# Differential attention: score matmuls over 128 rows, the next heads' projections asked for two token tiles earlier, and the products beside the attention paced evenly

## The chip, the cores and the metric

One core of a Trainium2 chip runs the whole program. The metric is the device time of one execution in microseconds (us), the median of several runs. The engines are TensorE (PE; its weight loads are listed apart as PEld), VectorE (DVE), ScalarE (ACT), GpSimd (POOL) and SyncE (SP). Each has a queue of its own that it works through in order; semaphores join them.

## The reference

The program is two transformer blocks on 512 tokens of width 1024, all in float32. The change lies in the first block's differential attention. Of the reference, what matters here (8 heads, `hd` = 64, so each head has two query and two key vectors of 64 per token and a value of 128):

```python
q = rmsnorm(q.reshape(bsz, s, B_HEADS, 2, B_HEAD_DIM), q_norm_g[l])
k = rmsnorm(k.reshape(bsz, s, B_HEADS, 2, B_HEAD_DIM), k_norm_g[l])
...
sc = jnp.einsum('bhcqd,bhckd->bhcqk', qb, k) * scale
alibi = -slopes[:, None, None] * jnp.abs(dist)[None]
sc = jnp.where((dist >= 0)[None, None, None], sc + alibi[None, :, None], -jnp.inf)
p = jax.nn.softmax(sc, axis=-1)
a = p[:, :, 0] - lam * p[:, :, 1]
return jnp.einsum('bhqk,bhkd->bhqd', a.astype(v.dtype), v)
```

q, k and v are columns of one projection `h @ w_in`. The output gate `sigmoid(h @ w_gate + b_gate)` is needed after the attention and needs nothing of it.

## The kernel before, in words

**Precise products.** Matrix operands are split into a rounded high part and a low remainder (`split_to`, lines 232 to 239: ACT writes the high part, DVE subtracts for the low one), and a product is three matmuls (`mm3`, lines 299 to 302: high times high, high times low, low times high).

**The list of dense products.** Products with weights are put on a list, an object of class `Dense` called `dn`. An item is one weight tile of 1 MB; it is loaded by SP, split by ACT and DVE (lines 290 and 291) and used in two "groups". A group of `dense_N` is 48 matmuls of 256 columns and counts as 48 x 109 = 5232 ns, one of `dense_T` is 24 matmuls of 512 columns and counts as 24 x 216 = 5184 ns. These counts are a budget and not measured times. `dn.run(ns)` adds to a debt and emits groups until the debt is paid; `dn.until(name)` emits groups until a named item is done, whatever the debt; `dn.drain()` emits the rest. The emitted program is then put in order for each engine by a scheduler, so matmuls of a group can stand between other work.

**The projections of two heads.** `push_qkv(hp)` (line 601) lists three products of 256 columns for heads 2hp and 2hp+1: q, k and v, two groups each. `evq` normalises q or k on DVE (`group_norm`, line 366: a square on ACT, then a sum, ten small operations of `rsqrt` and a multiplication on DVE). `lay(which)` (line 617) transposes the result on PE and splits it into the tile `qk`. For one head `qk` had five slots of 512 columns on 128 partitions. Slots 0 and 1 are q of the two components c: its high part in its own 64 partitions, its low part in the other 64. Slots 2 and 3 are k of the two components: the high part in its own 64 partitions, and a copy of it in the other 64, which POOL makes with a DMA (line 631). Slot 4 holds the low parts of k, component 0 in partitions 0 to 63, component 1 in 64 to 127.

**One step of the attention.** There are 32 steps, i = 0 to 31: head h = i // 4, token tile qt = i % 4 with n = 128 (qt + 1) keys. `scores(i)` issues two matmuls for each component: line 669 over all 128 rows (q high and q low, each times k high) and line 670 over the component's own 64 rows (q high times k low). `soft` adds the position term, finds the row minimum (line 680, DVE), takes the exponential (line 682, ACT) and combines the two components (lines 685 to 688, DVE). `turn` transposes (line 381) and copies (line 695), `values` multiplies with v (line 705). On PE the step i issues scores(i), turn(i-1) and values(i-2), with a `yield` after the first two; at each yield the caller runs `dn.run`.

**What sets the order beside it.** Before the attention the projections of the first two heads are done (`until("qkv0")`). The list then holds, in this order, qkv1, gate 0, qkv2, gate 1, qkv3, gate 2, gate 3 (a gate item, `push_gate_b`, is one `dense_T` tile of two groups). Each of the yields pays 1150 ns. `scores` calls `dn.until` for the projections of a pair of heads at that pair's first step. POOL's queue also holds `bn` (line 659), the position term of one head, in two buffers: a new one waits until DVE has read the head before last.

**After it** come `up_b` (the product with w_up_b, which needs all heads), the output product, the mixture of experts, whose weight buffers are granted as the output product proceeds, and the second block.

Of the kernel before, what the change touches and what calls it, by code (L numbers as in the profile page):

```python
# [6 lines left out]
F32 = mybir.dt.float32  # L7
F32R = mybir.dt.float32r
# [8 lines left out]
S = 512  # L17
# [142 lines left out]
def _body(ctx, tc, I, out):  # L160
# [270 lines left out]
                       channel_multiplier=1)  # L431
    cols = cp.tile([128, 128], F32, name="cols")
    C = {}
    b_bc = c1.tile([128, 8, 128], F32, name="b_bc")
    wsT = c1.tile([128, 8, 128], F32, name="wsT")
    nlam = cp.tile([128, 1], F32, name="nlam")
    hb_gate = cp.tile([128, 16], F32, name="hb_gate")
    g_sub = cp.tile([128, 1], F32, name="g_sub")
# [81 lines left out]
    T2["p"] = sub(gs, "t2", 7)  # L520
    v_n = gp.tile([128, 4, 1024], F32, name="v_n")
    yaT = [gp.tile([128, 8, S], F32R, name=f"yaT{i}") for i in range(2)]
    cg = constants(gp)

    def gn2(c, q, ps):
# [75 lines left out]
    def push_qkv(hp):  # L601
        qkn = {}
        h = HQ[hp] = {}

        def evq(which):
            def ev(c, q, ps):
                x = t2("qkn", (128, 2, 4, 64))
                group_norm(ps.rearrange("p (g w) -> p g w", w=64), x.rearrange("p t g w -> p (t g) w"), 8, 64)
                qkn[which, q] = x
            return ev  # L610

        def evv(c, q, ps):
            if q == 0:
                h["vb"] = ap_.tile([128, 4, 256], F32, name="vb", tag="vb")
            act.activation(h["vb"][:, 2 * q:2 * q + 2], ps.rearrange("p (t w) -> p t w", t=2), AF.Copy)

        def lay(which):
            def f():
                dn.flush()
                if which == 0:  # L620
                    h["qk"] = ap_.tile([128, 10, S], F32R, name="qk", tag="qk")
                g = col("k_norm_g") if which else g_q
                for j in range(2):
                    ps = transpose4(lambda t: qkn[which, t // 2][:, t % 2, 2 * j:2 * j + 2].rearrange("p a b -> p (a b)"))
                    for c in range(2):
                        own, other = halves(c)
                        hi = h["qk"][:, 5 * j + 2 * which + c]
                        lo = h["qk"][own, 5 * j + 4] if which else hi[other]
                        split_to(hi[own], lo, ps[own], g[own])
                        if which:  # L630
                            pool.dma_start(hi[other], hi[own])
            return f
        dense_N(w_in, 2048 + hp * 256, 256, lambda: hT, evq(0))
        dense_N(w_in, 3072 + hp * 256, 256, lambda: hT, evq(1))
        dn.call(lay(0))
        dense_N(w_in, 4096 + hp * 256, 256, lambda: hT, evv)
        dn.call(lay(1))
        dn.call(lambda: None, f"qkv{hp}")
# [10 lines left out]
    def attention():  # L649
        st = {}  # L650
        n_steps = 32

        def scores(i):
            h, qt = divmod(i, 4)
            if qt == 0 and h % 2 == 0:
                dn.until(f"qkv{h // 2}")
            if qt == 0:
                bn = c1.tile([128, 512], F32, name="bn", tag="bn", bufs=2)
                pool.tensor_scalar(bn, dpos, slopes[h], None, op0=OP.mult)
                st["bn"] = bn  # L660
            qk = HQ[h // 2]["qk"][:, 5 * (h % 2):5 * (h % 2) + 5]
            n = 128 * (qt + 1)
            nm = max(n, 256)
            qs = slice(qt * 128, qt * 128 + 128)
            pss = []
            for c in range(2):
                own = halves(c)[0]
                ps = psa()
                pe.matmul(ps[:, :nm], qk[:, c, qs], qk[:, 2 + c, :nm], start=True, stop=False)
                pe.matmul(ps[:, :nm], qk[own, c, qs], qk[own, 4, :nm], start=False, stop=True)  # L670
                pss.append(ps)
            return pss, n, qt, st["bn"]

        def soft(a):
            pss, n, qt, bn = a
            mn, den, rd = small("mn", [128, 2], 6), small("den", [128, 2], 6), small("rd", [128, 2], 6)
            sc = []
            for c in range(2):
                s = t2("sc")
                dve.tensor_tensor_reduce(s[:, :n], pss[c][:, :n], bn[:, 384 - 128 * qt:512], 1.0, 3.0e38,  # L680
                                         op0=OP.add, op1=OP.min, accum_out=mn[:, c:c + 1])
                act.activation(s[:, :n], s[:, :n], AF.Exp, bias=mn[:, c:c + 1], scale=-1.0,
                               accum_out=den[:, c:c + 1])
                sc.append(s)
            dve.reciprocal(rd, den)
            dve.tensor_mul(rd[:, 1:2], rd[:, 1:2], nlam)
            dve.tensor_scalar(sc[0][:, :n], sc[0][:, :n], rd[:, 0:1], None, op0=OP.mult)
            dve.scalar_tensor_tensor(sc[0][:, :n], sc[1][:, :n], rd[:, 1:2], sc[0][:, :n], op0=OP.mult, op1=OP.add)
            return sc[0], n, qt

        def turn(a):
            s, n, qt = a
            pt = transpose4(lambda k: s[:, k * 128:k * 128 + 128], qt + 1)
            aT = t2("aT")
            act.activation(aT[:, :n], pt[:, :n], AF.Copy)
            return aT

        def values(i, aT):
            h, qt = divmod(i, 4)
            vb = HQ[h // 2]["vb"]  # L700
            if qt == 0:
                st["po"] = psa()
            po = st["po"]
            for kt in range(qt + 1):
                pe.matmul(po[:, qt * 128:qt * 128 + 128], aT[:, kt * 128:kt * 128 + 128],
                          vb[:, kt, (h % 2) * 128:(h % 2) * 128 + 128], start=kt == 0, stop=kt == qt)
            if qt == 3:
                on = t2("on", (128, 4, 128))
                group_norm(po.rearrange("p (g w) -> p g w", g=4), on, 4, 128)
                st["on"] = (h, on)  # L710

        def finish():
            h, on = st.pop("on")
            ps = transpose4(lambda t: on[:, t])
            act.activation(ybT[:, h], ps, AF.Copy, scale=g_sub)

        sc, aT = {}, {}
        for i in range(n_steps + 3):
            fin = "on" in st
            if i < n_steps:  # L720
                sc[i] = soft(scores(i))
            yield
            if 1 <= i <= n_steps:
                aT[i - 1] = turn(sc.pop(i - 1))
            yield
            if fin:
                finish()
            if 2 <= i <= n_steps + 1:
                values(i - 2, aT.pop(i - 2))

    push_qkv(0)
    dn.until("qkv0")
    push_qkv(1)
    push_gate_b(0)
    push_qkv(2)
    push_gate_b(1)
    push_qkv(3)
    push_gate_b(2)
    push_gate_b(3)
    for _ in attention():  # L740
        dn.run(1150.0)
    dn.drain()
    at_.close()
    hs_.close()
# [1298 lines left out]
```

## Time and profile before

| | |
|---|---|
| median of 3 runs | 1792.62 us (1791.51 to 1793.68) |
| the profiled execution, its own time | 1795.56 us |
| its span, first to last instruction | 1793.5 us |
| mean granted TensorE clock | 0.972 of full speed |
| PE busy | 1692.7 us (94% of the span) |
| PEld busy | 1373.6 us (77%) |
| DVE busy | 947.6 us (53%) |
| ACT busy | 662.1 us (37%) |
| POOL busy | 285.7 us (16%) |

Busy PE is not PE at its peak, because matmuls are pipelined: a matmul's duration in the trace is longer than its distance to the next one. What a matmul costs is read from start to start. Durations on DVE overlap a little as well. "Granted clock" is the share of the full TensorE clock of 2.4 GHz in a stretch, so 0.5 is the lower level, 1.2 GHz. The attention lies between about 248 and 482 us of the span.

### The profile page before, as it was taken

The page shows a single profiled execution, that of the slowest core. Times are in us where ns is not written, and L with a number is a line of the kernel's source. Part 1 is how long each engine was busy: PE and PEld are TensorE (multiplying, and loading weights), DVE is VectorE, ACT ScalarE, POOL GpSimd, SP SyncE. Part 2 cuts the span into 40 slices and gives each one's busy share as a digit, 9 for nine tenths or more (in the row PEclk, how much of TensorE's full clock was granted, in tenths as well). Part 3 has the DMA queues.
Part 4 walks back from the last instruction along what each step waited for, and adds up shares of the span by engine and source line. Part 5 has one row for each costly group of instructions (what it writes and reads, how often), then busy time and mean ns, then how long its engine had stood idle before and what let it go on. Part 6 is the DMA issues. An engine that isn't in the chain of part 4 may idle for free.

```text
span 1793.5 us, 24558 instructions
## 1 busy us (share of the span) xinstructions
PE 1692.7 (94%) x9766; PEld 1373.6 (77%) x9766; DVE 947.6 (53%) x2001; ACT 662.1 (37%) x1128; POOL 285.7 (16%) x276
## 2 busy tenths in 40 slices
PE   7999999999999699887799988799999999999999
PEld 7888888889789455444789876588788988888887
DVE  7642367777753411111578789964467444444221
ACT  4222244454523122122435577566523322222111
POOL 1000000000012222112200178611001111111000
PEclk9999999999999799899899999899999999999999
DMA  6223322122348899998724311121243222222240
GB/s 205 94 71 117 118 84 82 48 83 83 141 141 314 324 411 415 418 416 298 218 94 118 118 48 47 71 94 48 88 142 122 83 94 94 94 94 94 83 141 35
DMA packets 151018, 263.87 MB, mean 147 GB/s; under 512 B 11771, under 2 KB 109766, under 8 KB 146550
## 3 DMA queue, kind: packets, MB, share of 16 engines
q1 hardware_dynamic: 131542, 220.03, 34.2%
q0 software_dynamic: 12400, 33.71, 6.1%
q10 hardware_dynamic: 6960, 8.56, 1.3%
q8 instruction: 77, 1.26, 0.3%
q14 instruction: 39, 0.32, 0.1%
HBM read 248.62 MB, written 18.87 MB: 149 GB/s over the span
## 4 chain that ended last, share of the span: by engine, by line
PE 41%; DVE 7%; ACT 2%; DMA 2%; issue 1%; POOL 0%; ACTq 0%; DVEq 0%; POOLq 0%
PE pd L300 11%; PE pd L301 11%; PE pd L302 11%; DVE oa L1756 3%; PE pa L301 2%; PE pa L300 2%; PE pa L302 2%; DMA x<-y_d 2%; DVE wlo L291 1%; PE pa L381 1%; PE pa L1646 1%; ACT whi L290 1%; DVE sn L1661 0%; DVE sden L1668 0%; DVE pt L236 0%
## 5 line engine op out<-in xcount | busy, mean ns | idle before, releaser
L291 DVE TENSOR_TENSOR wlo<-wraw,whi 128x2048 fp32r<-128x2048 f32 (+1 forms) x112 | 248.8, 2221 | 192.8 <-ACT whi L290 192.1
L290 ACT ACTIVATE whi<-wraw 128x2048 fp32r<-128x2048 f32 (+1 forms) x123 | 213.1, 1735 | 345.8 <-PE pd L301 198.8
L301 PE MATMUL pd<-wlo,hT 128*128 128x256 f32 x512 | 145.5, 284 | 1.5 <-DVE wlo L291 1.5
L300 PE MATMUL pd<-whi,hT 128*128 128x256 f32 x512 | 146.0, 285 | 0.0
L302 PE MATMUL pd<-whi,hT 128*128 128x256 f32 x512 | 145.2, 284 | 0.0
L302 PE MATMUL pd<-hnT,wlo 128*128 128x512 f32 x352 | 139.4, 396 | 0.0
L300 PE MATMUL pd<-hnT,whi 128*128 128x512 f32 x352 | 139.3, 396 | 0.0
L301 PE MATMUL pd<-hnT,whi 128*128 128x512 f32 x352 | 139.2, 395 | 0.0
L300 PE MATMUL pd<-xnT,whi 128*128 128x512 f32 (+1 forms) x280 | 114.3, 408 | 0.0
L301 PE MATMUL pd<-xnT,whi 128*128 128x512 f32 (+1 forms) x280 | 113.0, 404 | 0.0
L302 PE MATMUL pd<-xnT,wlo 128*128 128x512 f32 (+1 forms) x280 | 112.9, 403 | 0.0
L1750 POOL TENSOR_TENSOR oa<-oa,ctm 128x512 f32<-128x512 f32 x60 | 91.3, 1522 | 60.5 <-ACT ctm L1749 57.0
L301 PEld LDWEIGHTS pd<-wlo,hT 128*128 128x128 f32 x512 | 97.2, 190 | 2.6 <-DVE wlo L291 1.8
L300 PEld LDWEIGHTS pd<-whi,hT 128*128 128x128 f32 x512 | 97.4, 190 | 1.2 <-issue 0.9
L302 PEld LDWEIGHTS pd<-whi,hT 128*128 128x128 f32 x512 | 97.1, 190 | 0.9 <-issue 0.4
L870 DVE SCALAR_TENSOR_TENSOR sg<-sg,pd 128x256 f32<-128x256 f32 x16 | 6.7, 421 | 165.6 <-ACT sg L869 165.6
L891 PE MATMUL pd<-mraw,xs 128*64 128x256 f32 x624 | 77.6, 401 | 11.8 <-DMA mraw<-in_w 11.6
L300 PEld LDWEIGHTS pd<-hnT,whi 128*128 128x128 f32 x352 | 66.1, 188 | 16.0
L301 PEld LDWEIGHTS pd<-hnT,whi 128*128 128x128 f32 x352 | 66.1, 188 | 15.9
L302 PEld LDWEIGHTS pd<-hnT,wlo 128*128 128x128 f32 x352 | 66.1, 188 | 15.8
L300 PE MATMUL pd<-hT,whi 128*128 128x512 f32 x192 | 77.8, 405 | 0.0
L302 PE MATMUL pd<-hT,wlo 128*128 128x512 f32 x192 | 77.7, 405 | 0.0
(546 smaller groups left out, 4059.1 us busy)
## 6 DMA issues: line engine op xcount, KB each, us to landing
mraw<-in_w SPq DMA_DIRECT2D x59, 1024.0 KB
wraw<-in_w_in SPq DMA_DIRECT2D x41, 1024.0 KB
wraw<-in_w_gate SPq DMA_DIRECT2D x19, 1024.0 KB
wraw<-in_w SPq DMA_DIRECT2D x11, 1024.0 KB
wraw<-in_w_up SPq DMA_DIRECT2D x11, 1024.0 KB
wlo<-in_w SPq DMA_DIRECT2D x10, 1024.0 KB
whi<-in_w SPq DMA_DIRECT2D x10, 1024.0 KB
wraw<-in_w_down SPq DMA_DIRECT2D x10, 1024.0 KB
```

The source lines that it names most:

```text
L290: act.activation(h[:, sl], r[:, sl], AF.Copy)
L291: (pool if i in by_pool else dve).tensor_tensor(l[:, sl], r[:, sl], raw(h[:, sl]), op=OP.subtract)
L300: pe.matmul(ps, ah, bh, start=start, stop=False)
L301: pe.matmul(ps, ah, bl, start=False, stop=False)
L302: pe.matmul(ps, al, bh, start=False, stop=stop)
L381: pe.transpose(ps[:, t * 128:t * 128 + 128], src_of(t), ident)
L870: dve.scalar_tensor_tensor(sg, sg, 1.0, hid[:, 0:256], op0=OP.add, op1=OP.mult)
L891: pe.matmul(ph[64 * m:64 * m + 64, 256 * j:256 * j + 256], XS[p][:, kt, 64 * m:64 * m + 64], wt[:, m, k], start=kt == 0, stop=kt == 7)
L1646: pe.matmul(ps[:, :nm], Q[:, 4 * g + i, qs], KS[:, br, g, x, :nm], start=x == 0, stop=x == 1)
L1750: pool.tensor_add(acc, acc, tm)
L1756: taps.append(lambda i=i: dve.scalar_tensor_tensor(acc, up[:, j, i:i + S], convw[:, i, j:j + 1], acc, op0=OP.mult, op1=OP.add))
```

## The change

The score matmul of line 670 becomes one over all 128 rows. `qk` gets six slots for each head: the low part of k has a slot for each component, in the component's own 64 partitions, and POOL's DMA copies high and low part together to the other 64. The second matmul then also adds q low times k low. The room comes from two tiles (`b_bc`, `wsT`) that now live only as long as the gating stage that reads them. The list is put as qkv1, qkv2, qkv3 and then the four gate items; a yield pays 2250 ns for the first 44 of 70 yields and 1550 ns after them. `dn.until` for the next pair is called at token tile 2 of a pair's second head, two steps before the pair begins.

```diff
-    b_bc = c1.tile([128, 8, 128], F32, name="b_bc")
-    wsT = c1.tile([128, 8, 128], F32, name="wsT")
...
+    b_bc = gp.tile([128, 8, 128], F32, name="b_bc")
+    wsT = gp.tile([128, 8, 128], F32, name="wsT")
...
-                    h["qk"] = ap_.tile([128, 10, S], F32R, name="qk", tag="qk")
+                    h["qk"] = ap_.tile([128, 12, S], F32R, name="qk", tag="qk")
...
-                        hi = h["qk"][:, 5 * j + 2 * which + c]
-                        lo = h["qk"][own, 5 * j + 4] if which else hi[other]
+                        hi = h["qk"][:, 6 * j + 2 * which + c]
+                        lo = h["qk"][own, 6 * j + 4 + c] if which else hi[other]
                         split_to(hi[own], lo, ps[own], g[own])
                         if which:
-                            pool.dma_start(hi[other], hi[own])
+                            both = h["qk"][:, 6 * j + 2 + c:6 * j + 5 + c:2]
+                            pool.dma_start(both[other], both[own])
...
-            if qt == 0 and h % 2 == 0:
-                dn.until(f"qkv{h // 2}")
+            if qt == 2 and h % 2 == 1 and h < 7:
+                dn.until(f"qkv{h // 2 + 1}")
...
-            qk = HQ[h // 2]["qk"][:, 5 * (h % 2):5 * (h % 2) + 5]
+            qk = HQ[h // 2]["qk"][:, 6 * (h % 2):6 * (h % 2) + 6]
...
             for c in range(2):
-                own = halves(c)[0]
                 ps = psa()
                 pe.matmul(ps[:, :nm], qk[:, c, qs], qk[:, 2 + c, :nm], start=True, stop=False)
-                pe.matmul(ps[:, :nm], qk[own, c, qs], qk[own, 4, :nm], start=False, stop=True)
+                pe.matmul(ps[:, :nm], qk[:, c, qs], qk[:, 4 + c, :nm], start=False, stop=True)
...
     push_qkv(0)
     dn.until("qkv0")
-    push_qkv(1)
-    push_gate_b(0)
-    push_qkv(2)
-    push_gate_b(1)
-    push_qkv(3)
-    push_gate_b(2)
-    push_gate_b(3)
-    for _ in attention():
-        dn.run(1150.0)
+    for hp in range(1, 4):
+        push_qkv(hp)
+    for c in range(4):
+        push_gate_b(c)
+    for i, _ in enumerate(attention()):
+        dn.run(2250.0 if i < 44 else 1550.0)
```

How this moves instructions, at two places. The first is PE at the beginning of the third pair of heads (head 4). Before, in PE's order, with `qkn` the normalised q or k, `hT` the block's input, `vb` the values and `sc` a softmax result:

```order
L302 MATMUL pd<-whi,hT_74 128x256
L381 MATMUL pa<-ident,qkn 128x128 x8
L705 MATMUL pa<-vb,aT 128x128 x3
L300 MATMUL pd<-hT_73,whi 128x512
...
L669 MATMUL pa<-qk 128x256
L670 MATMUL pa<-qk 128x256
L302 MATMUL pd<-hT_73,wlo 128x512
```

and in the changed kernel the same eight transposes of k for that pair, which now stand at token tile 1 of head 3 (the L669 and L670 rows here are that tile's scores):

```order
L302 MATMUL pd<-whi,hT_74 128x256
L705 MATMUL pa<-vb,aT 128x128 x3
L669 MATMUL pa<-qk 128x256
L670 MATMUL pa<-qk 128x256
L669 MATMUL pa<-qk 128x256
L670 MATMUL pa<-qk 128x256
L381 MATMUL pa<-ident,sc 128x128
L381 MATMUL pa<-ident,qkn 128x128 x8
L300 MATMUL pd<-whi,hT_73 128x256
```

Before, eleven matmuls of a gate product lay between the transposes of k and the first scores that need them; now three steps of the attention with their dense products lie between (L669 of head 4 follows 125 rows later).

The second place is POOL's queue over the whole attention (`bn` is the position term of a head, `qk` the copies of k). Before:

```order
L659 TENSOR_SCALAR bn<-dpos 128x512 x2
L631 DMA qk<-qk 64x512 x4
L659 TENSOR_SCALAR bn<-dpos 128x512 x2
L631 DMA qk<-qk 64x512 x4
L659 TENSOR_SCALAR bn<-dpos 128x512 x2
L631 DMA qk<-qk 64x512 x4
```

(from the terms of heads 2 and 3 on, to the copies of the last pair), and now, from the copies of the first pair on:

```order
L632 DMA qk<-qk 64x2x512 x4
L660 TENSOR_SCALAR bn<-dpos 128x512
L632 DMA qk<-qk 64x2x512 x4
L660 TENSOR_SCALAR bn<-dpos 128x512 x2
L632 DMA qk<-qk 64x2x512 x4
L660 TENSOR_SCALAR bn<-dpos 128x512 x2
L632 DMA qk<-qk 64x2x512 x4
L660 TENSOR_SCALAR bn<-dpos 128x512
```

The copies of a pair now stand ahead of the position term of the running pair's second head; before, they stood behind it. Each copy moves twice the bytes.

## Rows read from the trace of the kernel before

**Rows 1.** Windows: from:to us, length, busy PE, PEld, DVE, ACT, POOL, then PEclk, DMA share, GB/s.
```profile
247.80:482.40 234.60, 230.43 (x1475) 195.79 (x1475) 170.22 (x525) 115.18 (x240) 19.65 (x26) 0.98 0.24 72
```

**Rows 2.** Timeline of PE, token tile 3 of head 2: start, us, engine, line, what.
```profile
322.17 0.47 PE L669 MATMUL pa<-qk 128*128 128x512 f32 x1
322.57 0.50 PE L670 MATMUL pa<-qk 64*128 64x512 f32 x1
323.00 0.50 PE L669 MATMUL pa<-qk 128*128 128x512 f32 x1
323.44 0.49 PE L670 MATMUL pa<-qk 64*128 64x512 f32 x1
323.86 0.39 PE L300 MATMUL pd<-whi,hT 128*128 128x256 f32 x1
```

**Rows 3.** Timeline of the weight loads at the same place; in brackets the idle time before.
```profile
322.57 0.18 PEld L670 LDWEIGHTS pa<-qk 64*128 64x128 f32 x1 [0.24 <-issue]
323.00 0.19 PEld L669 LDWEIGHTS pa<-qk 128*128 128x128 f32 x1 [0.25 <-issue]
323.97 0.19 PEld L301 LDWEIGHTS pd<-wlo,hT 128*128 128x128 f32 x1
```

**Rows 4.** Timeline of PE, scores of 256 columns and what follows.
```profile
271.18 0.36 PE L669 MATMUL pa<-qk 128*128 128x256 f32 x1
...
272.41 0.33 PE L381 MATMUL pa<-ident,sc 128*128 128x128 f32 x1
```

**Rows 5.** Timeline of PE, second block: four score matmuls over 128 rows.
```profile
1186.51 1.09 PE L1646 MATMUL pa<-KS,Q 128*128 128x512 f32 x4
1187.44 0.39 PE L300 MATMUL pd<-omT,whi 128*128 128x512 f32 x1
```

**Rows 6.** Timeline of PE, a dense product resumed after value matmuls.
```profile
285.48 0.37 PE L301 MATMUL pd<-wlo,hT 128*128 128x256 f32 x1
285.69 0.28 PE L302 MATMUL pd<-whi,hT 128*128 128x256 f32 x1
285.81 0.28 PE L300 MATMUL pd<-whi,hT 128*128 128x256 f32 x1
```

**Rows 7.** Line 670 over the run: min/median/max ns, first and last start, forms.
```profile
L670 PE MATMUL pa<-qk x64: 377/439/686, 248.1 to 473.9; 64*128 64x256 f32 x32, 64*128 64x384 f32 x16, 64*128 64x512 f32 x16
```

**Rows 8.** Timeline of PE: where it waited; in brackets the wait and its releaser.
```profile
247.81 0.35 PE L669 MATMUL pa<-qk 128*128 128x256 f32 x1 [1.20 <-ACT qk L238]
298.75 0.66 PE L381 MATMUL pa<-ident,qkn 128*128 128x128 f32 x4 [0.39 <-DVE qkn L374]
308.11 0.36 PE L669 MATMUL pa<-qk 128*128 128x256 f32 x1 [1.78 <-DMA qk<-qk]
```

**Rows 9.** Windows of 10 us, same columns as rows 1.
```profile
280.00:290.00 10.00, 10.00 (x78) 9.03 (x77) 8.13 (x25) 5.49 (x10) 0.00 (x0) 1.00 0.32 106
290.00:300.00 10.00, 9.61 (x77) 8.96 (x76) 9.07 (x25) 7.82 (x13) 1.49 (x1) 1.00 0.01 2
300.00:310.00 10.00, 8.22 (x36) 5.87 (x34) 4.65 (x9) 3.86 (x9) 2.12 (x4) 0.97 0.59 157
310.00:320.00 10.00, 10.00 (x28) 7.25 (x29) 6.61 (x28) 2.09 (x7) 0.00 (x0) 0.52 0.00 0
```

**Rows 10.** Timeline of DVE while k of the first pair is laid out.
```profile
244.14 1.40 DVE L239 SCALAR_TENSOR_TENSOR qk<-pa,cols,qk 64x512 fp32r<-64x512 f32 x2 [4.33 <-ACT qk L238]
246.51 2.29 DVE L291 TENSOR_TENSOR wlo<-wraw,whi 128x2048 fp32r<-128x2048 f32 x1 [0.98 <-ACT whi L290]
248.84 1.43 DVE L239 SCALAR_TENSOR_TENSOR qk<-pa,cols,qk 64x512 fp32r<-64x512 f32 x2
```

**Rows 11.** Timeline of POOL at the same place.
```profile
244.65 1.07 POOL L631 DMA_DIRECT2D qk<-qk  x2 [35.07 <-ACT qk L238]
```

**Rows 12.** DMA issues: what, queue, count, KB each, median us to landing.
```profile
qk<-qk POOLq DMA_DIRECT2D x16, 128.0 KB, 2.8
```

**Rows 13.** Groups of DVE by line, attention stage: busy us, mean ns, idle before.
```profile
L374 DVE TENSOR_TENSOR qkn<-pd,grr 128x512 f32<-128x512 f32 x12 | 8.3, 692 | 0.7
L372 DVE TENSOR_REDUCE gss<-sq 128x8 f32<-128x512 f32 x12 | 8.1, 678 | 2.9 <-ACT sq L371 2.9
L358 DVE TENSOR_TENSOR rs_a<-grr 128x8 f32<-128x8 f32 x12 | 2.0, 168 | 0.4
```

## The prediction

> **What bounds the kernel now.** I went first to the stage that the change touches, the attention, in the view of windows, because a share over the whole span mixes stages. From the first scores to the first product after the attention 234.6 us pass, and PE is busy for 230.4 of them, DVE for 170.2 (73%), ACT for 115.2 [rows 1]. PE idles for little, so PE sets the length here, and what counts is how closely its instructions follow one another. For that I took the timeline of PE, start to start. Three things stand out.
>
> First, the scores are dear. The four score matmuls of token tile 3, 512 columns each, start at 322.17, 322.57, 323.00 and 323.44, and the next product at 323.86: 1.69 us, 0.42 each [rows 2]. Four score matmuls of the second block, with the same 512 columns but 128 rows in all four, take 0.93 us, 0.23 each [rows 5]. The weight loads show why: where line 670 (64 rows) follows line 669 (128 rows), or the reverse, the load begins only when its own matmul begins, after 0.24 or 0.25 us without a load; a load between matmuls of 128 rows (323.97) starts well before its matmul and shows no such gap [rows 3]. So each change of the row count leaves a load of 0.18 us uncovered.
>
> Second, at the beginning of the second pair of heads PE waits 1.78 us for the DMA that copies k [rows 8], and after that the granted clock of 310 to 320 us is 0.52, almost wholly the lower level (1.2 GHz), with 28 matmuls in 10 us where the windows before had 78 and 77 [rows 9].
>
> Third, DVE is not far behind: 9.07 of 10 us at 290 to 300, where a projection runs beside the attention [rows 9].
>
> **The change part by part.**
>
> *Scores over 128 rows.* The number of matmuls and columns stays. A step of 512 columns costs 1.69 us now; at the distance of the second block's it costs 0.93. One cost stays: the first of the four mostly follows value matmuls, and a matmul that resumes after those takes 0.21 us to the next instead of 0.12 [rows 6], so I add 0.09: 1.02, a gain of 0.67. A step with 256 columns takes 1.23 us now, 271.18 to 272.41 [rows 4]; three matmuls at 0.12 and one at 0.21 make 0.57 [rows 6], a gain of 0.66. The 384-column steps I put at 0.67, between equal neighbours. The forms count 32, 16 and 16 matmuls of line 670 [rows 7], two a step, so 16, 8 and 8 steps: 10.6 + 5.4 + 5.4 = **21.4 us off**. All of it is on the path, since PE sets the length. Bounds: 24.3 if the 0.09 goes too (32 x 0.09 = 2.9), 0 if row count is not the cause.
>
> A rule speaks against this. The Trainium skill ("TensorE: Matmul & The Clock Gate", what overlaps and what doesn't, in its part on packing small matmuls) says that a weight load overlaps a running matmul only when their row groups differ. By it loads among 128-row matmuls would stay uncovered and the term would be 0. The trace does not agree: the 0.23 us of four 128-row matmuls in a row [rows 5] leaves no room for an uncovered 0.18.
>
> *Projections two tiles earlier.* The transposes, splits and copies are the same, only placed ahead of three steps of the attention. The 1.78 us wait goes, and the 0.39 us for a normalised k [rows 8]: **2.2 us off**. With the wait goes, I expect, the slow stretch behind it: 10 us at 0.52 and 10 us at 0.97 lose 4.8 + 0.3 = **5.1 us** [rows 9]. Bounds: 0 and 7.3 for both. What is late next is nothing on POOL: the copies no longer stand behind the position term that waits for the running pair to end, so they go out as soon as DVE has split k.
>
> *Larger copies.* A copy now waits for DVE's low part too, and carries 256 KB. In the middle of the attention three steps cover it. At the first pair nothing does: PE already waits 1.20 us there [rows 8]; the first copies, issued at 244.65 [rows 11], must wait for splits that end by 245.54, and the second component's until 250.27, behind a weight split of 2.29 us [rows 10]. Landing took 2.8 us for 128 KB [rows 12]; twice the bytes takes between 2.8 and 5.6. The order of the change puts 14 more dense matmuls (14 x 0.12 = 1.7 us) ahead of the first score. I take **1.5 us on**, between 0 and 5. DMA itself is idle for three quarters of the stage [rows 1].
>
> *Even pacing and the list's order.* No instruction comes or goes. The forced stretches of pure projection before pairs 3 and 4 spread out, and DVE's work with them. Without contention the stage is 234.6 - 21.4 - 7.3 + 1.5 = 207.4 us, so DVE would be busy 82% of it. But the first 22 of 32 steps now hold all three projections. PE there: 44 x 2.25 = 99 us of budget are 18.9 groups of 48 matmuls at 0.12, 109 us; the remaining 36.7 of the 135.7 us budget are 7.1 groups of 24 at 0.23, 39 us; 207.4 less both leaves 59 us of the attention's own, 1.85 a step, so 22 steps take 109 + 41 = 150 us. DVE there: a projected pair costs three weight splits of 2.29, eight splits of 0.72 [rows 10], and four norms of 0.68 + 0.69 + 10 x 0.17 [rows 13], 25 us, so 75 for three; the rest of 170.2, less five weight splits of the later products (11), is 84 over 32 steps, 2.6 a step, 58 in 22. With one gate split, 135 us, 90% of PE's 150. That is the share of the window at 290, where PE lost 0.39 us [rows 9]. With both engines so full some waits must come. Bounds: 0, if DVE keeps its 0.907; 16, if it only sustains the 0.813 of the window at 280 (135 / 0.813 = 166). I take **4 us on**, nearer the 290 window because there DVE had more to do.
>
> *The moved tiles* (`b_bc`, `wsT`) change no instruction: 0. *What follows* starts from events of the attention's end, its weights wait for buffers that the output product frees, so it moves forward as a block: 0.
>
> **Sum.** -21.4 - 2.2 - 5.1 + 1.5 + 4 = -23.2 us. The profiled execution took 1795.56, so 1772.4 for its like; it lies 2.9 above the median of 1792.62, which gives **1769.4 us**. About 0.2%, 3.6 us, is what a measurement of this kernel can tell from no change.
>
> **The rivals.**
>
> *DVE becomes the bound.* For it: 135 of 150 us, and in-order queues on both sides. Against it: 9.07 of 10 was reached. At 0.813 the loss is 16 instead of 4: 1781.4. With the start's upper bound, 1785.
>
> *Row count is not the cause* (the rule above, or the change of row groups is priced elsewhere). The scores stay at 0.42, PE has 21 us more, so DVE has room: -7.3 + 1.5, 1787. Against it rows 3 and 5.
>
> *Slower: a starved PE loses its clock.* In the first 22 steps PE waits on DVE as it did on the DMA at 306, and each time a stretch at the lower level follows. One such spell costs 1.8 + 5.1 = 6.9 us; the gain without contention is 27.2, so from the fourth spell the change loses. Five give 1792.6 - 27.2 + 34.5 = 1799.9. For it: one wait of 1.78 sufficed. Against it: after the waits of 1.20 and 0.39 us [rows 8] the clock stayed, 1.00 at 290 to 300 [rows 9].
>
> **How the numbers follow.** The forecast, 1761 to 1776, has 0.66. Its lower end is 24.3 + 7.3 off with nothing added: 1761. DVE as the bound, 1776 to 1787, 0.20. Row count without effect 0.06, a third of which falls within 0.2%. The clock spells 0.05. Small effects that cancel 0.03. So faster 0.90, the same 0.05, slower 0.05. For 8 in 10 the range is the forecast and most of the DVE case: 1761 to 1784.
>
> **What would show it.** Right: the four scores of 512 columns start 0.23 us apart; no gap in the weight loads there; the wait for the copies at the second pair gone and no window at 0.52; DVE above 0.8 in the stage; the stage about 211 us long. Wrong: scores still 0.4 apart (first term); waits of PE on DVE (softmax results, split weights or normalised k) adding up to over 10 us before the fourth pair (last term); a granted clock near 0.5 behind such a wait.

## The result, and the profile after

| kernel | median us (runs) | ratio to before, 95% interval |
|---|---|---|
| before | 1792.07 (1791.26 to 1793.68, 4 runs) | |
| changed | 1774.32 (1772.46 to 1776.35, 4 runs) | 0.99 [0.9888, 0.9913] |

The change takes 17.75 us off, 1.0%. The forecast was 1769.4 us, with 1761 to 1784 as its range. The profiled execution of the changed kernel took 1774.05 us; that of before took 1795.56. So the two profiles differ by 21.5 us, 3.8 more than the medians do, and part of the account below goes to this difference.

The page of the changed kernel, span and busy time of the engines:

```profile
span 1772.2 us, 24544 instructions
PE 1664.7 (94%) x9766; PEld 1366.9 (77%) x9766; DVE 942.6 (53%) x2001; ACT 658.8 (37%) x1128; POOL 288.1 (16%) x276
```

Windows of the changed kernel: first the stage as in [rows 1], then 10 us each as in [rows 9] (from:to, length, busy PE, PEld, DVE, ACT, POOL, then PEclk, DMA share, GB/s):

```profile
249.98:463.00 213.02, 203.96 (x1461) 188.35 (x1461) 165.22 (x524) 112.00 (x240) 22.51 (x26) 0.99 0.33 88
250.00:260.00 10.00, 7.43 (x51) 7.26 (x52) 3.46 (x14) 2.21 (x8) 1.16 (x2) 0.87 0.69 162
260.00:270.00 10.00, 10.00 (x78) 9.83 (x77) 9.50 (x35) 4.98 (x11) 0.00 (x0) 0.96 0.18 58
...
300.00:310.00 10.00, 9.39 (x76) 8.84 (x75) 8.62 (x33) 5.88 (x16) 2.08 (x3) 1.00 0.67 107
310.00:320.00 10.00, 10.00 (x85) 10.00 (x85) 9.38 (x35) 4.60 (x10) 0.00 (x0) 1.00 0.32 106
```

The stage is 213.0 us long instead of 234.6. It begins 2.2 us later, about half of it because 14 more dense matmuls stand ahead of it (the transposes of the first k already begin at 243.6 instead of 242.6); so its end moves from 482.4 to 463.0, by 19.4. The window at 0.52 is gone: at 310 to 320 the clock is 1.00, while DVE is busy for 9.38 us. (The 85 matmuls there instead of 28 are not the clock alone: the dense ones have 256 columns now, and had 512 in that window before.) What is new is the dip to 0.87 and 0.96 at the beginning.

PE of the changed kernel: the waits at the start and, further on, four of the nine of over 0.2 us for DVE or ACT in the middle of the stage, as in [rows 8]; between them token tile 3 of head 2, the place of [rows 2]:

```profile
249.98 0.35 PE L669 MATMUL pa<-qk 128*128 128x256 f32 x1 [0.72 <-issue]
...
257.25 0.43 PE L669 MATMUL pa<-qk 128*128 128x256 f32 x1 [2.57 <-DMA qk<-qk]
...
301.79 0.63 PE L381 MATMUL pa<-ident,on 128*128 128x128 f32 x4 [0.30 <-DVE on L374]
...
324.54 0.47 PE L669 MATMUL pa<-qk 128*128 128x512 f32 x1
324.86 0.39 PE L670 MATMUL pa<-qk 128*128 128x512 f32 x1
325.08 0.40 PE L669 MATMUL pa<-qk 128*128 128x512 f32 x1
325.32 0.39 PE L670 MATMUL pa<-qk 128*128 128x512 f32 x1
325.55 0.28 PE L300 MATMUL pd<-whi,hT 128*128 128x256 f32 x1
...
328.01 0.66 PE L381 MATMUL pa<-ident,qkn 128*128 128x128 f32 x4 [0.47 <-DVE mn L680]
...
335.96 0.63 PE L381 MATMUL pa<-ident,sc 128*128 128x128 f32 x4 [0.93 <-DVE qk L239]
...
354.56 0.66 PE L381 MATMUL pa<-ident,on 128*128 128x128 f32 x4 [0.47 <-DVE on L374]
```

The weight loads at the four scores, as in [rows 3]:

```profile
324.51 0.19 PEld L669 LDWEIGHTS pa<-qk 128*128 128x128 f32 x1
324.63 0.19 PEld L670 LDWEIGHTS pa<-qk 128*128 128x128 f32 x1
324.86 0.19 PEld L669 LDWEIGHTS pa<-qk 128*128 128x128 f32 x1
325.09 0.19 PEld L670 LDWEIGHTS pa<-qk 128*128 128x128 f32 x1
```

Four scores of 512 columns take 1.01 us instead of 1.69. The distances are 0.32, 0.22, 0.24 and 0.23: 0.23 for all but the one that follows value matmuls. From the second on, each load begins within 0.1 us of the start of the matmul before it. By line over the whole run, as in [rows 7]:

```profile
L670 PE MATMUL pa<-qk x64: 278/334/420, 250.2 to 451.2; 128*128 128x256 f32 x32, 128*128 128x384 f32 x16, 128*128 128x512 f32 x16
```

The nine waits in the middle sum to 3.7 us. No pair but the first waits for its copies any more. At the first, the copies leave POOL in two groups, since a weight split stands between the two components' splits on DVE, as in [rows 10]. POOL's timeline of the changed kernel:

```profile
246.44 1.22 POOL L632 DMA_DIRECT2D qk<-qk  x2 [35.87 <-DVE qk L239]
250.88 1.25 POOL L632 DMA_DIRECT2D qk<-qk  x2 [3.22 <-DVE qk L239]
```

The second component's score starts 6.4 us after 250.88. Landing has grown, too: the median of the copies of [rows 12] was 2.8 us, and now the row of the DMA issues reads

```profile
qk<-qk POOLq DMA_DIRECT2D x16, 256.0 KB, 6.3
```

### The profile page after: what moved, and what is told of

Its sections match the earlier page's. It is cut to its first block, busy times and chain, and to the rows that moved or that the text cites. A ratio compares the mean times of both kernels' runs of the same rounds, so it can differ in the third digit from the quotient of the medians.

```text
span 1772.2 us, 24544 instructions
## 1 busy us (share of the span) xinstructions
PE 1664.7 (94%) x9766; PEld 1366.9 (77%) x9766; DVE 942.6 (53%) x2001; ACT 658.8 (37%) x1128; POOL 288.1 (16%) x276
## 4 chain that ended last, share of the span: by engine, by line
PE 73%; DVE 12%; DMA 9%; ACT 3%; issue 2%; POOL 0%; SPq 0%; DVEq 0%; POOLq 0%; ACTq 0%
PE pd L300 18%; PE pd L302 18%; PE pd L301 18%; PE pd L888 4%; PE pa L381 3%; DVE oa L1753 3%; DMA mraw<-in_w 3%; DVE wlo L291 2%; PE pa L301 2%; PE pa L300 2%; PE pa L302 2%; DMA y_d<-yt,dest 2%; PE pd L904 2%; DMA x<-y_d 2%; DMA wlo<-in_w 1%
## 5 line engine op out<-in xcount | busy, mean ns | idle before, releaser
L290 ACT ACTIVATE whi<-wraw 128x2048 fp32r<-128x2048 f32 (+1 forms) x123 | 213.0, 1734 | 346.9 <-PE pd L301 200.7
L888 PE MATMUL pd<-mraw,xs 128*64 128x256 f32 x624 | 74.9, 390 | 13.5 <-DMA mraw<-in_w 13.3
```

What stands on the lines that cost most here:

```text
L290: act.activation(h[:, sl], r[:, sl], AF.Copy)
L888: pe.matmul(ph[64 * m:64 * m + 64, 256 * j:256 * j + 256], XS[p][:, kt, 64 * m:64 * m + 64], wt[:, m, k], start=kt == 0, stop=kt == 7)
```

## The experiments

All times below are medians of timed runs, unless called a single execution; the ratio is to the kernel before, run on the same chip.

**The rows alone, and the order alone.** The first kernel has the 128 rows and the larger copies, but the list, the pacing and the place of the call as before:

```diff
 (against the changed kernel)
-            if qt == 2 and h % 2 == 1 and h < 7:
-                dn.until(f"qkv{h // 2 + 1}")
+            if qt == 0 and h % 2 == 0:
+                dn.until(f"qkv{h // 2}")
...
-        dn.run(2250.0 if i < 44 else 1550.0)
+        dn.run(1150.0)
```

(and the list qkv1, gate 0, qkv2, gate 1, qkv3, gates 2 and 3). The second kernel is its complement: the kernel before with the new list, pacing and call, and the scores over 64 rows as they were.

> Only the six slots, the larger copies and the 128-row second score matmul; list, pacing and the call for the next pair as in the kernel before. Theory (the rows carry the gain, the pacing hides the copies): four scores of 512 columns 0.23 us apart, 21 us off the scores, but the copies of twice the size are waited for at the start of all four pairs, 2 to 5 us each, so 8 to 17 us faster than the kernel before. Rival (the new order costs as much as it hides, and the rows alone are worth the whole): 18 us faster or more, at or below the changed kernel.

> Only the list, the pacing and the earlier call; scores over 64 rows as before. Theory: the wait for the copies at the second pair and what follows it go, PE still sets the length, 2 to 7 us faster than the kernel before. Rival (DVE, spread evenly, makes PE wait for as much as is hidden): within 2 us of the kernel before or slower.

Measured: the rows alone 1792.41 us, ratio 1.0004 [0.9995, 1.0013]; the order alone 1786.69 us, ratio 0.9971 [0.9961, 0.998], 4.8 us off. So the parts, 0 and 4.8, don't add up to the 17.75 of both. In the kernel with the rows alone the scores are as short as hoped: the distances from each of the 128 score matmuls to the next instruction sum to 25.3 us (45.8 before, 24.4 in the changed kernel). But the 20 us are all given back, so the theory (8 to 17 us faster) and the rival (18 or more) are both wrong in the time. PE of that kernel, four of its waits:

```profile
257.12 0.55 PE L669 MATMUL pa<-qk 128*128 128x256 f32 x1 [3.14 <-DMA qk<-qk]
347.11 0.38 PE L300 MATMUL pd<-whi,hT 128*128 128x256 f32 x1 [3.06 <-DVE qkn L374]
380.67 0.36 PE L669 MATMUL pa<-qk 128*128 128x256 f32 x1 [3.37 <-DMA qk<-qk]
447.49 0.55 PE L669 MATMUL pa<-qk 128*128 128x256 f32 x1 [3.74 <-DMA qk<-qk]
```

and the clock behind two of them:

```profile
250.00:260.00 10.00, 6.86 (x47) 6.69 (x46) 3.13 (x15) 2.08 (x8) 1.16 (x2) 0.81 0.69 158
260.00:270.00 10.00, 10.00 (x70) 9.83 (x69) 8.32 (x27) 4.68 (x9) 0.00 (x0) 0.85 0.01 2
340.00:350.00 10.00, 6.60 (x48) 6.21 (x47) 8.77 (x35) 3.59 (x8) 2.01 (x1) 0.92 0.32 106
350.00:360.00 10.00, 10.00 (x80) 10.00 (x80) 7.84 (x24) 4.80 (x6) 0.00 (x0) 0.91 0.01 2
```

These four waits make 13.3 us; the four windows lose 1.9 + 1.5 + 0.8 + 0.9 = 5.1 more in clock. All waits of PE of over 0.15 us, up to the first product after the attention, sum to 20.5 us here, against 5.4 before and 9.5 in the changed kernel. With the order alone, whose time is inside its theory, PE waits nowhere in the middle of the stage: the waits of 1.78 and 0.39 us [rows 8] are gone, and the window at 310 to 320, the slow one of before, reads

```profile
310.00:320.00 10.00, 10.00 (x79) 9.27 (x77) 9.27 (x37) 4.54 (x9) 0.00 (x0) 1.00 0.33 107
```

**Is it the row count?** Both score products over their own 64 rows, in the kernel before, each component on its own half:

```diff
 (against the kernel before)
-                pe.matmul(ps[:, :nm], qk[:, c, qs], qk[:, 2 + c, :nm], start=True, stop=False)
+                pe.matmul(ps[:, :nm], qk[own, c, qs], qk[own, 2 + c, :nm], start=True, stop=False)
```

> The kernel before with both score matmuls over the component's own 64 rows (the product of q low and k high is left out). Theory (a weight load is uncovered where the row group changes): inside a component the two matmuls of 512 columns stand 0.23 us apart, between components and at the ends 0.42, some 8 to 14 us off in all. Rival (a load of 64 rows is never covered): all four stay 0.40 to 0.44 apart, time as before within 4 us. Second rival (the rule of the skill: a load is covered only where row groups differ): 0.42 inside a component and 0.23 between the two.

A single execution: 1780.24 us, against 1791.5 of the kernel before. (Its scores read no copies any more; the waits sum to 5.3 us, as before.) The score distances sum to 21.2 us, less than over 128 rows. PE and its loads, four scores of 512 columns:

```profile
311.30 0.39 PE L705 MATMUL pa<-vb,aT 128*128 128x128 f32 x2
311.62 0.50 PE L669 MATMUL pa<-qk 64*128 64x512 f32 x2
311.96 0.40 PE L670 MATMUL pa<-qk 64*128 64x512 f32 x2
312.29 0.50 PE L302 MATMUL pd<-hT,wlo 128*128 128x512 f32 x1
```

```profile
311.62 0.19 PEld L669 LDWEIGHTS pa<-qk 64*128 64x128 f32 x2
311.73 0.19 PEld L670 LDWEIGHTS pa<-qk 64*128 64x128 f32 x2
312.29 0.19 PEld L302 LDWEIGHTS pd<-hT,wlo 128*128 128x128 f32 x1 [0.36 <-issue]
```

The 11 us off are inside the theory's 8 to 14, but the rows show something neither theory had: the matmuls of the two components start together. Four take 0.67 us where four over 128 rows take 0.93 [rows 5]. Each component alone goes at 0.33 to 0.34, but the other, on the other half of the rows, runs beside it. So the dear thing is the change between 128 and 64 rows that overlap (0.42), not 64 rows as such. It is still paid at the entry of each step: the first score starts 0.20 us after the last value matmul here, and 0.03 where the scores have 128 rows. Over the stage the distances from another matmul to a score (waits left out) sum to 11.6 us, against 3.2 before and 2.0 in the changed kernel. With them the scores cost 32.8 us here and 26.4 in the changed kernel: 128 rows are the cheaper way.

**How far do executions of one kernel differ?** Both kernels once more, unchanged.

> The kernel before once more, for its profile. Theory: the wait of about 1.8 us at the second pair and the stretch at half clock after it are there in every execution. Rival: the half clock is an accident of the one profiled execution, the clock stays 1.00 there and the span is some 3 to 5 us shorter than 1793.5.

> The changed kernel once more, for one look. Theory: the wait for the first pair's copies (2.57 us in its first profile) is part of the program's order and recurs, 2 to 3 us; the clock of 0.87 and 0.96 behind it is the execution's own and may be anywhere between 0.85 and 1.00. Rival: both recur within a few hundredths, and the start costs some 4 us in every execution. Time 1772 to 1777 us.

Before again: 1791.76 us, the wait for the copies, and the stretch behind it:

```profile
309.01 0.36 PE L669 MATMUL pa<-qk 128*128 128x256 f32 x1 [1.74 <-DMA qk<-qk]
```

```profile
310.00:320.00 10.00, 10.00 (x43) 7.59 (x42) 6.62 (x30) 3.33 (x10) 0.00 (x0) 0.83 0.00 0
```

The wait recurs (1.78 and 1.74), the clock behind it doesn't: 0.83 instead of 0.52, 1.7 us lost instead of 5.1. The changed kernel again: 1775.09 us, and

```profile
257.14 0.53 PE L669 MATMUL pa<-qk 128*128 128x256 f32 x1 [3.25 <-DMA qk<-qk]
```

```profile
250.00:260.00 10.00, 6.75 (x46) 6.58 (x45) 3.10 (x14) 2.22 (x8) 1.16 (x2) 0.86 0.67 157
260.00:270.00 10.00, 10.00 (x79) 9.83 (x78) 9.49 (x36) 4.98 (x11) 0.00 (x0) 0.97 0.19 58
```

Here the clock came out alike (0.87 and 0.96 before, 0.86 and 0.97 now), so the rival holds for this place: in both executions the start costs about the same. Between these two second executions the first product after the attention starts at 480.70 and 462.95: 17.75 us apart, which happens to be what the medians differ by (the whole times of these two are 16.7 apart).

**The start, and DVE's share.** The first pair's high and low parts copied by DMAs of their own, and a kernel with one constant pace instead of two:

```diff
 (against the changed kernel; first the copies, then, in another kernel, the pace)
-                            pool.dma_start(both[other], both[own])
+                            if hp:
+                                pool.dma_start(both[other], both[own])
+                            else:
+                                for e in range(2):
+                                    pool.dma_start(both[other, e], both[own, e])
...
-        dn.run(2250.0 if i < 44 else 1550.0)
+        dn.run(2000.0)
```

> The changed kernel, but for the first pair of heads the high and the low part of k are copied by two DMAs, the high part first. Theory (at the first pair nothing covers the larger copies; they cost a wait of 2.6 us and a stretch below full clock after it): the wait for the second component's copy shrinks to under 1.5 us, 1 to 4 us faster than the changed kernel, 1770 to 1773. Rival (the low part is as late as before, behind the weight split on DVE): the wait only moves to the second score matmul, same time as the changed kernel within 1 us, 1773 to 1776.

> The changed kernel with 2000 ns at every yield, so that the projections lie over more steps and DVE's share in the first 22 steps falls. Theory (DVE's fullness in the first part makes PE wait some 4 us): 1 to 3 us faster than the changed kernel, 1771 to 1773. Rival (those waits come from the order inside a step, not from DVE's share): same within 1 us, 1773 to 1776.

Copies apart: 1774.19 us, ratio 0.9912 [0.9898, 0.9925]. The wait for the second component shrank from 2.57 to 1.55 us, and it now stands at the second score matmul, the one that reads the low part (line 674), as the rival said; the wait at the first score grew from 0.72 to 1.33. In this execution the clock does not dip:

```profile
255.82 0.50 PE L674 MATMUL pa<-qk 128*128 128x256 f32 x2 [1.55 <-DMA qk<-qk]
```

```profile
250.00:260.00 10.00, 8.45 (x72) 8.24 (x71) 4.86 (x23) 2.57 (x9) 1.02 (x2) 1.00 0.55 146
260.00:270.00 10.00, 10.00 (x82) 9.83 (x81) 9.46 (x32) 4.67 (x10) 0.00 (x0) 1.00 0.34 107
```

In the profile the stage ends 2.3 us earlier (460.73), but the span is only 0.7 shorter (1771.5), and the median is that of the changed kernel. So the time is the rival's; whether some of the 2.3 us stays is below what these runs tell. The flat pace: 1774.05 us, ratio 0.9902 [0.9886, 0.9917], the same; three waits for DVE of 0.69 to 1.23 us stand where the smaller ones were. So the rival holds here too: these two paces give the same time.

**The early call without the new order.** The changed kernel with list and pacing of before, the call still two steps early:

> The changed kernel with the list and the pacing of before: 128-row scores and the earlier call remain. Theory (the earlier call alone hides the copies of pairs 2 to 4, which cost the rows-only kernel some 10 us of waits and slow clock): no wait for copies at those pairs, 1778 to 1785, between the rows alone and the changed kernel. Rival (what hides them is the even pacing, the call changes little): 1788 to 1793.

Measured: 1793.79 us, ratio 1.0017 [1.0008, 1.0026], slightly slower than before. The theory's 1778 to 1785 is wrong, and the rival (1788 to 1793) nearer. All four pairs wait for copies, 3.73, 2.30, 2.54 and 2.97 us, and near the end PE stands once for DVE:

```profile
372.63 0.39 PE L669 MATMUL pa<-qk 128*128 128x256 f32 x1 [2.54 <-DMA qk<-qk]
...
470.50 1.08 PE L381 MATMUL pa<-ident,on 128*128 128x128 f32 x4 [5.64 <-DVE on L374]
```

At this third pair the last two copies leave at 366.13, and 4.0 us later PE has nothing else to do. So the call by itself brings no cover; it takes the list and the pace as well. What the call adds to these was not tried apart. By their budget it has little to force: when it comes for the second pair, 12 yields have paid 27.0 us of the 31.4 that the pair's six groups count, and for the later pairs all is paid.

**What gave the 20 us back?** Three kernels take the copies out and put them in again. The scores are three products over 64 rows each (high by high, high by low, low by high), the two components on different halves, as the run on the row count suggests. q and k are split over 128 rows at once, so DVE and ACT have half the instructions for it, and nothing is copied:

```diff
 (against the changed kernel)
-                    for c in range(2):
-                        own, other = halves(c)
-                        hi = h["qk"][:, 6 * j + 2 * which + c]
-                        lo = h["qk"][own, 6 * j + 4 + c] if which else hi[other]
-                        split_to(hi[own], lo, ps[own], g[own])
-                        if which:
-                            both = h["qk"][:, 6 * j + 2 + c:6 * j + 5 + c:2]
-                            pool.dma_start(both[other], both[own])
+                    at = 4 * j + 2 * which
+                    split_to(h["qk"][:, at], h["qk"][:, at + 1], ps, g)
...
+            for e, (a, b) in enumerate(((0, 2), (0, 3), (1, 2))):
+                for c in range(2):
+                    own = halves(c)[0]
+                    pe.matmul(pss[c][:, :nm], qk[own, a, qs], qk[own, b, :nm], start=e == 0, stop=e == 2)
```

The first has the new order, the second list, pacing and call of before, and the third is the second with copies of k added, to other columns of the same rows, which the scores then read:

```diff
 (third against second)
+                    if which:
+                        for c in range(2):
+                            own = halves(c)[0]
+                            pool.dma_start(h["qk"][own, at + 2:at + 4], h["qk"][own, at:at + 2])
```

> The changed kernel with no copies at all: both components side by side in one slot of 128 partitions, high and low parts of q and k in four slots a head, each split for 128 partitions at once, and three products of 64 rows for each component (q high k high, q high k low, q low k high), components in turn; q low times k low is left out as in the kernel before. Theory (two 64-row matmuls in different halves of the rows run side by side, as in the run with 64 rows throughout; DVE loses 16 of 32 splits of 0.75 us and PE the waits for copies): a step of 512 columns takes about 1.0 us as now, 6 to 12 us faster than the changed kernel, 1762 to 1768. Rival (six matmuls with loads uncovered inside a half cost more than is saved): 1774 or slower.

> Scores as three products of 64 rows each, the two components on different halves and no copies of k at all, but list, pacing and call of the kernel before. Theory: what ate the gain of the scores when they alone were made over 128 rows (1792.4 us, no gain) were the waits for the copies, three of them with 10.2 us together, and the stretches at the lower clock behind them. Without copies these go, and of the 21 us some 10 to 17 stay: 1775 to 1782 us. Rival: the copies were only the place where it showed; with all dense products in the first half and projections forced before a pair, DVE (normalised k, splits) ends last there instead, and the time is 1787 us or more.

> The kernel with three products of 64 rows and the order of the kernel before (1775.4 us), with one thing added: k's high and low part are copied by four DMAs of 256 KB per pair to other columns of the same rows, and the scores read the copy. The products, the order and DVE's work stay. Theory: the copies by themselves ate the gain where only the rows were changed (1792.4 us); three or four waits of 2 to 4 us come back, with stretches at the lower clock, and the time is 1786 to 1794 us. Rival: the run without copies won because DVE's splits are wider and fewer there (about 8 us less DVE work in the stage); then the copies cost 6 us at most and the time is 1776 to 1782 us.

| scores | order | copies | us | ratio to before, 95% interval |
|---|---|---|---|---|
| 3 x 64 rows | new | none | 1774.55 | 0.9908 [0.9893, 0.9923] |
| 3 x 64 rows | before | none | 1775.43 | 0.9912 [0.9898, 0.9926] |
| 3 x 64 rows | before | 256 KB each | 1780.25 | 0.9928 [0.9914, 0.9941] |
| 2 x 128 rows | before | 256 KB each | 1792.41 | 1.0004 [0.9995, 1.0013] |
| 2 x 128 rows | new | 256 KB each | 1774.32 | 0.99 [0.9888, 0.9913] |

The score distances sum to 23.9 us in the first (24.4 in the changed kernel) and 24.5 in the second, but the distances into the scores sum to 7.1 and 8.7, against 2.0: at the entry of a step the change from 128 to 64 rows is paid again, so PE has some 5 to 7 us more to do than in the changed kernel. My expectation for the first fell: without copies and with less for DVE it is no faster than the change. PE's waits sum to 5.4 us instead of 9.5, and the entries take back what that gives. The time is the rival's, though the loads that cost it stand at the entry and not inside a half. The second, inside its theory, brings the same gain with the order of before, at a clock of 1.00 in every window of the stage. So the even order is not needed where no k has to be copied and DVE has half the splits. The third shows what the copies by themselves cost: 4.8 us by the medians, 2.9 by the ratios, whose intervals overlap (the two kernels ran on different chips). Either is inside the rival's 6. The other 12 us between it and the kernel with the rows alone are not PE's scores, which are dearer here (25.2 us and 8.6 into them, against 25.3 and 3.6). PE's waits sum to 4.6 us here and to 20.5 there, 10.2 of these for copies, and the rows show how the copies are fed. DVE and POOL of the kernel with the rows alone, at its third pair:

```profile
368.20 1.40 DVE L239 SCALAR_TENSOR_TENSOR qk<-pa,cols,qk 64x512 fp32r<-64x512 f32 x2 [4.34 <-ACT qk L238]
370.58 2.29 DVE L291 TENSOR_TENSOR wlo<-wraw,whi 128x2048 fp32r<-128x2048 f32 x1 [0.98 <-ACT whi L290]
372.91 1.43 DVE L239 SCALAR_TENSOR_TENSOR qk<-pa,cols,qk 64x512 fp32r<-64x512 f32 x2
```

```profile
369.24 1.25 POOL L632 DMA_DIRECT2D qk<-qk  x2 [25.85 <-DVE qk L239]
373.96 1.25 POOL L632 DMA_DIRECT2D qk<-qk  x2 [3.47 <-DVE qk L239]
```

and of the third kernel, at the same pair:

```profile
361.30 1.41 DVE L239 SCALAR_TENSOR_TENSOR qk<-pa,cols,qk 128x512 fp32r<-128x512 f32 x2 [6.22 <-ACT qk L238]
363.69 2.29 DVE L291 TENSOR_TENSOR wlo<-wraw,whi 128x2048 fp32r<-128x2048 f32 x1 [0.97 <-ACT whi L290]
```

```profile
362.35 2.13 POOL L630 DMA_DIRECT2D qk<-qk  x4 [26.34 <-DVE qk L239]
```

A split over 64 rows takes as long as one over 128 (0.7 us each). Split by halves, the second component falls behind a weight split, its copies leave 4.7 us after the first, and PE stands for 3.37 us. Split at once, all four copies leave together, and the waits of weight loads for them come to 1.3 us over all four pairs. (Where the rest of what the copies cost goes was not followed up.) The halves also cost DVE itself: line 239 is busy for 20.3 us in the stage of the one and 10.1 of the other. What this work and what the late copies cost apart was not tried, so that the way the copies are fed makes the 12 us is argued from these rows and not shown by a run.

## Why the prediction was right, and where it was off

- **Scores, -21.4.** In the two first profiles the distances shrink from 45.8 to 24.4 us: 21.4 off. In the two second ones from 44.5 to 24.5: 20.0. The 21.4 is met to the tenth partly by luck, since the 45.8 hold scores in the stretch at half clock, which the sum took off in another term. The price of a change of row count was read rightly from [rows 2, 3, 5]. By the rule that the prediction weighed (the Trainium skill, "TensorE: Matmul & The Clock Gate", what overlaps and what doesn't) loads among 128-row matmuls would stay uncovered; 0.23 us between the scores of 512 columns says again that they don't. That the rule's other half holds, loads and matmuls of different row groups overlapping, the kernel with 64 rows in both products shows: its two loads of line 669, on different halves, and both matmuls start at 311.62 to 311.63.
- **"All of it is on the path, since PE sets the length": the step that was too simple.** It holds for the whole change, and not for the rows alone, which gained nothing. PE set the length of the stage before because the scores were dear; once they are short, PE waits at three of the four pairs for copies that stand behind DVE's splits (3.1 to 3.7 us each), and the clock falls behind such waits. The prediction took larger copies as covered but for the first pair. This was right only because of the other parts of the change.
- **The waits, -2.2.** Both are gone. Right.
- **The half-clock stretch, -5.1: mis-sized.** It belonged to the one execution that was profiled. A second showed 1.7 us for the same wait. The stretch cost 3.4 us more in the profiled execution than in the second, which is likely part of why that one lay 2.9 us above the median (its stage was 2.7 us longer than the second's, and what follows the stage 2.0). The prediction took the whole stretch off, and then the 2.9 as well, so it took some of the same time off twice; without the second step its number was 1772.4. Its count of 28 matmuls against 78 overstates the stretch: those of 310 to 320 are mostly wider.
- **Larger copies, +1.5: too small.** PE waited 1.20 us at the start before; it waits 0.72 + 2.57 now, 2.1 more, and the clock of 0.87 and 0.96 loses 1.3 + 0.4: together 3.8. The bound of 5 held. Landing of 2.8 to 5.6 us was too low: the median is 6.3.
- **DVE's contention, +4.** The waits in the middle sum to 3.7 us. DVE kept up at 9.38 and 9.50 us of 10 [rows 9 for before: 9.07], so the rival in which it becomes the bound did not come. Over the stage its share is 0.78 (165.2 of 213.0 us): the sign "DVE above 0.8" was missed.
- **A starved PE that loses its clock.** It happened, in the kernels that have part of the change: with the rows alone four waits of 3.1 to 3.7 us, smaller ones and the clock ate the gain. In the whole change only the start is left of it.
- **What follows, 0.** From the first product after the attention on, the two first profiles take 1311.1 and 1309.2 us, the two second ones 1309.0 and 1310.2. It moved as a block, within 2 us.

With the sizes of the two first profiles: -21.4 - 2.2 - 5.1 + 3.8 + 3.7 = -21.2, where the stage ends 19.4 us earlier. With those of the two second ones: -20.0 - 2.1 - 1.7 + 4.0 + 3.6 = -16.2, where it ends 17.75 earlier. The terms account for the change to within 2 us and no closer, since a score in a slow stretch counts in two of them.

## What to carry to other kernels

Price a matmul by the distance of starts, and see whether neighbours in the order use overlapping but different rows: that, here 0.19 us each, is worth removing by equal rows. Disjoint halves remove it among themselves and keep it towards their 128-row neighbours. Work taken off the engine that sets the length is gained only as far as its inputs come earlier too, so follow each input (split, copy, landing) back, and see what stands in front of its last piece on its queue; one operation over all 128 rows instead of two over halves both shortened that queue and let the copies leave together. A stretch at a lower clock in one profile may be that execution's alone: read a second execution before counting it.

## What the hardware did that I had not expected

- Two matmuls over different halves of the rows start within 0.01 us of each other, and four of 512 columns take 0.67 us; on one half by itself the next starts after 0.33 to 0.34, so there a part of the load of 0.19 us stays uncovered.
- After the same wait of 1.7 to 1.8 us for the same DMA, the granted clock of 310 to 320 us was 0.52 in one execution and 0.83 in another, while the dip at the start of the changed kernel repeated within 0.01.
- A copy of k of 256 KB landed after 6.3 us (median) in the changed kernel, 4.0 in the one with the rows alone and 4.8 in the one with added copies; 128 KB took 2.8.
